# First-phase modulation in bursts of four tiles and raw transposes of x in a Hymba-style decoder block

## The chip, the cores and the metric

One core of a Trainium2 chip. The metric is the device time of one execution in microseconds, of the only core. All data is float32.

## The reference

One decoder layer on 256 tokens of width 2048. What matters here is its opening:

```python
mod = silu(c) @ W_ada + b_ada        # 6 x 2048: shift1, scale1, gate1, shift2, scale2, gate2
h   = RMSNorm(x, w1) * (1 + scale1) + shift1
u, q, k, v = split(h @ W_in)         # 1024 columns each
y_ssm = S5 diagonal SSM (64 groups of 16 channels, 64 states), GELU, GLU
y_att = QK-norm, dilated sliding-window attention with ALiBi (8 heads of 128)
x = x + gate1 * (concat(y_ssm, y_att) @ W_out)
x = x + gate2 * SwiGLU(RMSNorm(x, w2) * (1 + scale2) + shift2)
```

RMSNorm divides each token by the root of its mean square: one factor per row of x, which commutes with a transpose if it is then applied along the other axis.

## The kernel before

Every weight is read once, in tiles of 128 partitions x 1024 values (524,288 bytes), through one ring of six buffers (`raw`, line 105; `RAW = 6`). `load` (lines 104 to 107) takes the next ring buffer and issues the transfer on SyncE. SyncE's queue keeps the order in which the program issues; the other engines' orders are made ahead of the run by a scheduler that goes by program order and priorities (`tc.high_priority` moves a block forward). Once made, an engine's order is fixed.

A matmul weight is split into two parts, `whi` (ScalarE, line 131) and `wlo` (VectorE, line 133), and multiplied in three passes.

The opening, from the start to about 182 us, interleaves four things:

- The modulation of the first norm. `ada_stream` (lines 210 to 275) goes through sets p = 0 to 7; a set gives shift1 and scale1 for 256 channels and reads eight tiles, four of each kind. The tile is the moving operand and a four-column slice of silu(c) (`c7`) the weights (line 231). Tiles come in steps of two: load two, multiply both, yield. After the last step the sums go to SBUF (line 243), and after the first step of the next set `ada_finish` (lines 194 to 208) turns them into columns with four small matmuls (`adac`, line 199), adds bias and norm weight into `gcol` (lines 203 to 206) and calls `make_h(p)`. Sets of 512 columns, kinds 3 and 4 of the second norm, follow in the same stream.
- x. `x_norm` (lines 312 to 335): x lies in two tiles of the pool tag "x" (two buffers); sums of squares on ScalarE, 1/rms by a Newton iteration on VectorE (`rsqrt`, lines 89 to 100), both tiles scaled, then 32 transposes into PSUM (line 331) and eight copies of 128 x 512 into `xnT`.
- The projection. `make_h_(p)` (lines 588 to 596) makes 256 channels of h, transposed and in two parts, in a quarter of the pool tag "act" (four buffers, two p's each); `u_units` (lines 600 to 618) multiplies them with three tiles of W_in: two for u (line 608, into the PSUM tiles `uacc`) and one for the first half of q (line 150, `q0`).
- Constants and tables of the SSM on VectorE and ScalarE: `s5_consts` (line 354), `ssm_rot` (475) and `ssm_tables` (502), which need the transfer `bct <- bc` (line 668).

The main loop (lines 665 to 679) calls `ada` once in each turn n, steps the tables by a budget of 1.2 us, and from turn 9 on runs 1.45 units of the projection. A set takes eight turns, a p ten units. At turn 8 it fetches three tiles of W_in ahead, at turn 10 it issues bc:

```python
    for n in range(66):
        next(ada)
        if n == NBC:
            SP.dma_start(bct.rearrange("p a b c -> p (a b c)"), bc)
```

`U` takes one of x's two buffers (line 647) and is filled from `uacc` after p = 7 (`u_copy`, lines 649 to 654); `te` of `ssm_rot(2)` takes the other. Behind the opening come the rest of the in-projection with SSM and attention in between (to about 386 us), W_out, and the feed-forward part from about 523 us.

The second norm (lines 1026 to 1036) already uses the form of the change: `f = (x1T * g2) * rsw` with 1/rms as a row `rsw`, then Identity with a bias for the high part and one VectorE operation for the low part.

Of the kernel before, what the change touches and what calls it, by code (L numbers as in the profile page):

```python
# [7 lines left out]
F32 = mybir.dt.float32  # L8
F32R = mybir.dt.float32r
I32 = mybir.dt.int32  # L10
AF = mybir.ActivationFunctionType
ALU = mybir.AluOpType
# [3 lines left out]
D = 2048  # L16
# [45 lines left out]
def body(tc, sm, tabs, bc, brow, x, wada, wg2, win, wglu, wout, wgate, wup, wdown, out):  # L62
# [20 lines left out]
    A.dma_start(smt, sm)  # L83
    col = lambda n: smt[:, COLS[n][0]:COLS[n][1]]
# [89 lines left out]
    A.activation(cs, col("c"), AF.Tanh, scale=0.5)  # L174
    V.tensor_scalar(out=cs, in0=cs, scalar1=0.5, scalar2=0.5, op0=ALU.mult, op1=ALU.add)
    V.tensor_tensor(out=cs, in0=cs, in1=col("c"), op=ALU.mult)
    c7 = p1.tile([128, 16, 7], F32, name="c7")
    V.memset(c7, 0.0)
    V.tensor_copy(c7[:, :, 3], cs)  # L179
# [12 lines left out]
    h_hook = []  # L192

# [16 lines left out]
    def ada_stream(sets):  # L210

        pend = None
        for parts in sets:
            ps = ada_ps
            last = len(parts) - 1
            steps = []
            for i, (kind, g0, ng) in enumerate(parts):
                steps += [(i, h) for h in range(0, 2 * ng, 2)]
            w = parts[0][2] * 128
            nk = 1024 // w  # L220
            nt = 16 // nk
            seen = set()
            for n, (i, h) in enumerate(steps):
                kind, g0, ng = parts[i]
                base = kind * 4 + g0 // 4, (g0 % 4) // ng * nt + h
                wts = [load(wada[base[0], base[1] + t]).rearrange("p k n -> p (k n)") for t in range(2)]
                for t in (1, 0):
# [11 lines left out]
                if n < len(steps) - 1:  # L239
                    yield  # L240
# [66 lines left out]
    xt = [xp.tile([128, D], F32, name=f"x{t}", tag="x", bufs=2) for t in range(2)]  # L307
    for t in range(2):
        A.dma_start(xt[t], x[t])
    xnT = []  # L310

    def x_norm():
        ss1 = p1.tile([128, 2], F32, name="ss1")
        for t in range(2):
            junk = P8([128, D], "junk")
            A.activation(junk, xt[t], AF.Square, accum_out=ss1[:, t:t + 1])
            yield
        V.tensor_scalar(out=ss1, in0=ss1, scalar1=1.0 / D, scalar2=EPS, op0=ALU.mult, op1=ALU.add)
        rs1 = rsqrt(p1, ss1, 2, "a")
        yield  # L320
        V.tensor_scalar(out=xt[0], in0=xt[0], scalar1=rs1[:, 0:1], scalar2=None, op0=ALU.mult)
        A.mul(xt[1], xt[1], rs1[:, 1:2])
        yield
        for h in range(2):
            xn = P8([128, 8, 256], f"xnT{h}")
            for q in range(4):
                ps = ms([128, 2, 256], "tp")
                for k in range(2):
                    kc = h * 8 + q * 2 + k
# [3 lines left out]
                if q % 2:  # L333
                    yield
# [903 lines left out]
```

## Time and profile before

| what | us |
|---|---|
| median of 3 runs (lowest, highest) | 1264.25 (1263.53, 1267.47) |
| the profiled execution, its own time | 1264.14 |
| its span, first to last instruction | 1262.4 |
| TensorE busy in the span | 1216.4 |
| VectorE busy | 790.5 |
| ScalarE busy | 570.5 |
| mean granted TensorE clock | 0.996 |

The profile is one execution. The span is what the trace covers; the time of an execution has a little around it. Engines are PE (TensorE; PEld its weight loads), DVE (VectorE), ACT (ScalarE), POOL (GpSimd) and SP (SyncE, which issues transfers). A float32 matmul leaves two records. A line such as `L608 PE MATMUL uacc<-hT,whi` names the kernel's line, the engine, the operation, and its output and inputs. `[4.33 <-ACT hT L142]` says that the engine stood idle for 4.33 us before it and what ended the wait. Idle time of an engine that is not the bottleneck costs nothing.

### The profile page before, as it was taken

What the parts mean: (1) busy time and instruction counts of PE and PEld (TensorE: products, weight loads), DVE (VectorE), ACT (ScalarE), POOL (GpSimd) and SP (SyncE); (2) the same over time, 40 slices, a digit from 0 to 9 for tenths busy, and PEclk for the clock granted to TensorE, in tenths of its full rate; (3) what the DMA queues carried; (4) which work ended last, traced back from release to release, by engine and by line L of the source; (5) the groups of instructions that cost most, each with busy time, mean ns of one, the idle gap of its engine ahead of it and who ended that gap; (6) DMA issues with size and microseconds to landing.
All of it is one profiled execution on the core that took longest, in us unless ns stands there. A gap on an engine that the chain in (4) does not pass through costs nothing.

```text
span 1262.4 us, 18076 instructions
## 1 busy us (share of the span) xinstructions
PE 1216.4 (96%) x6884; PEld 965.2 (76%) x6884; DVE 790.5 (63%) x1389; ACT 570.5 (45%) x859; POOL 25.2 (2%) x50
## 2 busy tenths in 40 slices
PE   4888999999999999999999999999999999999998
PEld 2555667677789877688888888888888878888886
DVE  7894356667778989865655665665555444545443
ACT  3564373445455554554444444444434443333432
POOL 0210000000000000000000000000000000000000
PEclk9899999999999999999999999999999999999999
DMA  8788886777687799567777777777766556667662
GB/s 338 275 285 319 318 318 239 262 251 272 221 322 237 266 317 330 202 188 241 237 238 235 230 239 240 238 236 229 244 201 191 185 169 194 208 194 213 190 212 68
DMA packets 83032, 302.74 MB, mean 240 GB/s; under 512 B 9248, under 2 KB 9664, under 8 KB 82304
## 3 DMA queue, kind: packets, MB, share of 16 engines
q1 hardware_dynamic: 80784, 294.69, 70.4%
q10 hardware_dynamic: 1728, 4.38, 0.9%
q0 software_dynamic: 432, 2.51, 0.5%
q8 instruction: 54, 0.88, 0.3%
q14 instruction: 34, 0.28, 0.1%
HBM read 299.44 MB, written 2.10 MB: 239 GB/s over the span
## 4 chain that ended last, share of the span: by engine, by line
PE 80%; DVE 9%; DMA 6%; ACT 3%; issue 2%; SPq 0%; DVEq 0%; ACTq 0%
PE ff L150 38%; PE dn L150 14%; PE qkv L150 8%; PE dnl L150 5%; DMA raw<-wada 3%; PE ada L231 3%; PE uacc L608 3%; DVE wlo L133 2%; PE y L732 2%; DMA raw<-win 1%; DVE gate L268 1%; PE q L150 1%; PE y L728 1%; PE z L919 1%; PE S L698 1%
## 5 line engine op out<-in xcount | busy, mean ns | idle before, releaser
L133 DVE TENSOR_TENSOR wlo<-raw,whi 128x1024 fp32r<-128x1024 f32 x365 | 445.7, 1223 | 325.8 <-ACT whi L131 325.0
L131 ACT CAST whi<-raw 128x1024 fp32r<-128x1024 f32 x365 | 384.4, 1053 | 511.1 <-PE ff L150 268.6
L150 PE MATMUL ff<-whi,h2T 128*128 128x512 f32 x1408 | 437.2, 390 | 0.7 <-DVE h2T L1034 0.5
L150 PEld LDWEIGHTS ff<-whi,h2T 128*128 128x128 f32 x1408 | 264.0, 188 | 56.8 <-DVE h2T L1034 0.9
L150 PE MATMUL ff<-wlo,h2T 128*128 128x512 f32 x704 | 274.1, 389 | 0.0
L150 PE MATMUL dn<-whi,aT 128*128 128x512 f32 x528 | 163.4, 390 | 0.0
L150 PEld LDWEIGHTS ff<-wlo,h2T 128*128 128x128 f32 x704 | 132.2, 188 | 27.1
L150 PEld LDWEIGHTS dn<-whi,aT 128*128 128x128 f32 x528 | 99.1, 188 | 21.1 <-ACT whi L131 0.2
L150 PE MATMUL qkv<-whi,hT 128*128 128x512 f32 x320 | 107.4, 402 | 0.1
L150 PE MATMUL dn<-wlo,aT 128*128 128x512 f32 x264 | 103.1, 391 | 0.0
L231 PE MATMUL ada<-raw,c 128*4 128x256 f32 (+1 forms) x736 | 68.9, 470 | 16.1 <-DVE c L179 9.5
L150 PEld LDWEIGHTS qkv<-whi,hT 128*128 128x128 f32 x320 | 59.8, 188 | 25.1 <-issue 9.0
L1092 DVE SCALAR_TENSOR_TENSOR gate<-raw,cs,gate 128x1024 f32<-128x1024 f32 x32 | 41.1, 1285 | 56.5 <-DMA raw<-wg 56.5
L608 PE MATMUL uacc<-hT,whi 128*128 128x256 f32 x256 | 55.0, 308 | 9.4 <-ACT whi L131 4.9
L150 PE MATMUL qkv<-wlo,hT 128*128 128x512 f32 x160 | 63.6, 397 | 0.4 <-DVE wlo L133 0.4
L608 PEld LDWEIGHTS uacc<-hT,whi 128*128 128x128 f32 x256 | 42.5, 202 | 21.2 <-issue 9.5
L150 PEld LDWEIGHTS dn<-wlo,aT 128*128 128x128 f32 x264 | 49.6, 188 | 10.6 <-issue 0.5
L150 PE MATMUL dnl<-whi,aT 128*128 128x512 f32 x176 | 54.4, 389 | 0.0
L268 DVE SCALAR_TENSOR_TENSOR gate<-raw,cs,gate 128x512 f32<-128x512 f32 x64 | 47.8, 749 | 6.7 <-DMA raw<-wada 5.8
L231 PEld LDWEIGHTS ada<-raw,c 128*4 128x4 f32 x736 | 13.9, 87 | 42.5 <-issue 14.7
L608 PE MATMUL uacc<-hT,wlo 128*128 128x256 f32 x128 | 38.3, 300 | 1.1 <-DVE wlo L133 0.8
L150 PEld LDWEIGHTS dnl<-whi,aT 128*128 128x128 f32 x176 | 33.0, 188 | 7.0 <-DVE o L341 0.2
(312 smaller groups left out, 1262.1 us busy)
## 6 DMA issues: line engine op xcount, KB each, us to landing
raw<-wada SPq DMA_DIRECT2D x160, 512.0 KB, 5.3
raw<-wgate SPq DMA_DIRECT2D x88, 512.0 KB, 4.5
raw<-wup SPq DMA_DIRECT2D x88, 512.0 KB, 4.3
raw<-wdown SPq DMA_DIRECT2D x88, 512.0 KB, 4.3
raw<-win SPq DMA_DIRECT2D x64, 512.0 KB, 5.4
raw<-wout SPq DMA_DIRECT2D x32, 512.0 KB, 4.8
raw<-wg SPq DMA_DIRECT2D x32, 512.0 KB, 4.3
raw<-wglu SPq DMA_DIRECT2D x8, 512.0 KB, 4.8
```

Source lines behind the costliest of these rows:

```text
L131: A.copy(hi, raw)
L133: V.tensor_tensor(out=lo, in0=raw, in1=hi.bitcast(F32), op=ALU.subtract)
L150: PE.matmul(ps[t] if type(ps) is list else ps[:, t], lhsT=lhs(a, t), rhs=w[:, j], start=first and n == 0, stop=last and n == 2)
L231: PE.matmul(ps[32 * q:32 * q + 4, 0:w], lhsT=c7[:, kc, 3 - i:7 - i], rhs=wts[t][:, j * w:(j + 1) * w], start=q not in seen, stop=n == len( ...
L268: V.scalar_tensor_tensor(out=gb, in0=wt[:, j], scalar=cs[:, 2 * h + j:2 * h + j + 1], in1=gb, op0=ALU.mult, op1=ALU.add)
L608: PE.matmul(uacc[b][:, c], lhsT=wt[:, j, w], rhs=h[:, j, a], start=(kc == 0 and n == 0 and c % 2 == 0), stop=(kc == 15 and n == 2), skip_g ...
L698: PE.matmul(S[:, e, Q], lhsT=wv[:, 0, Q, e].rearrange("p i c -> p (i c)"), rhs=U[:, m, Q], start=True, stop=True)
L728: PE.matmul(yq[:, r], lhsT=T[:, Q, r], rhs=U[:, m, Q], start=r == 0, stop=False, skip_group_check=True, tile_position=(0, 32 * Q))
L732: PE.matmul(yq[:, r], lhsT=Vt[:, Q, e, r], rhs=hp[:, e, Q], start=False, stop=e == 1, skip_group_check=True, tile_position=(0, 32 * Q))
L919: PE.matmul(z[:, c], lhsT=wt[:, j, w], rhs=yT[kc // 4][:, kc % 4, a], start=(kc == 0 and n == 0 and c % 2 == 0), stop=(kc == 7 and n == 2) ...
L1092: V.scalar_tensor_tensor(out=g, in0=wt, scalar=cs[:, k:k + 1], in1=g, op0=ALU.mult, op1=ALU.add)
```

## The change

- The loads of x are issued right behind `smt`, ahead of the tanh on ScalarE's queue; silu(c) is made with high priority.
- A first-phase set takes its eight tiles in two steps of four instead of four steps of two, with the same eight turns. Of each four, two go through the ring, and the other two into one buffer of the tags "act" or "x" (`EXTRA`): "act" for the first step of sets 0 to 6 and the second step of sets 0 to 2, "x" for the second step of sets 3 to 7. The first step of set 7 takes four ring buffers. The matmuls of a step go from the last tile to the first.
- x is transposed as it came, through `uacc`, sixteen transposes at a time with four copies of 128 x 1024 in all; 1/rms becomes a row in all partitions (`rsx`) by two diagonal matrices, two matmuls with ones and a copy. `make_h_` applies it: two operations for the high part and one for the low part, for each of the two blocks of 128 channels.
- `U` is taken when `u_copy` first runs.

```diff
--- before.py
+++ after.py
@@ -81,6 +81,9 @@
 
     smt = const.tile([128, NSM], F32, name="smt")
     A.dma_start(smt, sm)
+    xt = [xp.tile([128, D], F32, name=f"x{t}", tag="x", bufs=2) for t in range(2)]
+    for t in range(2):
+        A.dma_start(xt[t], x[t])
     col = lambda n: smt[:, COLS[n][0]:COLS[n][1]]
     ident = col("id")
     ones = const.tile([128, 128], F32, name="ones")
@@ -171,12 +174,13 @@
 
 
     cs = const.tile([128, 16], F32, name="cs")
-    A.activation(cs, col("c"), AF.Tanh, scale=0.5)
-    V.tensor_scalar(out=cs, in0=cs, scalar1=0.5, scalar2=0.5, op0=ALU.mult, op1=ALU.add)
-    V.tensor_tensor(out=cs, in0=cs, in1=col("c"), op=ALU.mult)
     c7 = p1.tile([128, 16, 7], F32, name="c7")
     V.memset(c7, 0.0)
-    V.tensor_copy(c7[:, :, 3], cs)
+    with tc.high_priority(offset=HH):
+        A.activation(cs, col("c"), AF.Tanh, scale=0.5)
+        V.tensor_scalar(out=cs, in0=cs, scalar1=0.5, scalar2=0.5, op0=ALU.mult, op1=ALU.add)
+        V.tensor_tensor(out=cs, in0=cs, in1=col("c"), op=ALU.mult)
+        V.tensor_copy(c7[:, :, 3], cs)
     ada_ps = ms_p.tile([128, 512], F32, name="ada", bufs=1)
     V.memset(ada_ps, 0.0)
     sel = p1.tile([128, 4], F32, name="sel")
@@ -190,6 +194,13 @@
 
     MOD = {0: ("sh1", "bsh1", None), 1: ("g1", "bsc1", "w1"), 3: ("sh2", "bsh2", None), 4: ("g2", "bsc2", "w2")}
     h_hook = []
+
+    def EXTRA(si, n):
+
+        if n == 0 and si < 7:
+            return act, "act", 4
+        if n == 1:
+            return (act, "act", 4) if si < 3 else (xp, "x", 2)
 
     def ada_finish(parts, ev, whole=False):
         kind, g0, ng = parts[0]
@@ -210,21 +221,32 @@
     def ada_stream(sets):
 
         pend = None
-        for parts in sets:
+        for si, parts in enumerate(sets):
             ps = ada_ps
             last = len(parts) - 1
-            steps = []
-            for i, (kind, g0, ng) in enumerate(parts):
-                steps += [(i, h) for h in range(0, 2 * ng, 2)]
             w = parts[0][2] * 128
             nk = 1024 // w
             nt = 16 // nk
+            nb = 4 if nk == 4 else 2
+            steps = []
+            for i, (kind, g0, ng) in enumerate(parts):
+                steps += [(i, h) for h in range(0, nt, nb)]
             seen = set()
             for n, (i, h) in enumerate(steps):
                 kind, g0, ng = parts[i]
                 base = kind * 4 + g0 // 4, (g0 % 4) // ng * nt + h
-                wts = [load(wada[base[0], base[1] + t]).rearrange("p k n -> p (k n)") for t in range(2)]
-                for t in (1, 0):
+                wts = []
+                for t in range(nb):
+                    src = wada[base[0], base[1] + t]
+                    home = EXTRA(si, n) if nk == 4 and t >= 2 else None
+                    if not home:
+                        wts.append(load(src).rearrange("p k n -> p (k n)"))
+                        continue
+                    if t == 2:
+                        pr_ = home[0].tile([128, 2, 1024], F32, name="rawp", tag=home[1], bufs=home[2])
+                    SP.dma_start(pr_[:, t - 2], src)
+                    wts.append(pr_[:, t - 2])
+                for t in reversed(range(nb)):
                     for j in range(nk):
                         kc = (h + t) * nk + j
                         q = kc % 4
@@ -236,7 +258,7 @@
                     with tc.high_priority(offset=HH):
                         ada_finish(*pend)
                     pend = None
-                if n < len(steps) - 1:
+                for _ in range(nb - 1 if n < len(steps) - 1 else nb - 2):
                     yield
             ev = T2([128, 512], "adaev")
             with tc.high_priority(offset=HH):
@@ -304,35 +326,38 @@
         return next(ada, None) or 0.0
 
 
-    xt = [xp.tile([128, D], F32, name=f"x{t}", tag="x", bufs=2) for t in range(2)]
-    for t in range(2):
-        A.dma_start(xt[t], x[t])
     xnT = []
+    rsx = p2.tile([128, 256], F32, name="rsx", tag="hd", bufs=1)
 
     def x_norm():
+
         ss1 = p1.tile([128, 2], F32, name="ss1")
-        for t in range(2):
-            junk = P8([128, D], "junk")
-            A.activation(junk, xt[t], AF.Square, accum_out=ss1[:, t:t + 1])
+        for h in range(2):
+            xn = P8([128, 8, 256], f"xT{h}")
+            for t in range(2):
+                for i in range(2):
+                    for k in range(4):
+                        kc = h * 8 + i * 4 + k
+                        PE.transpose(uacc[i][:, k, t * 128:(t + 1) * 128], xt[t][:, kc * 128:(kc + 1) * 128], ident)
+                if h == 0:
+                    junk = P8([128, D], "junk")
+                    A.activation(junk, xt[t], AF.Square, accum_out=ss1[:, t:t + 1])
+                    yield
+            for i in range(2):
+                (V.tensor_copy if i else A.copy)(xn[:, 4 * i:4 * i + 4], uacc[i])
+            xnT.append(xn)
             yield
-        V.tensor_scalar(out=ss1, in0=ss1, scalar1=1.0 / D, scalar2=EPS, op0=ALU.mult, op1=ALU.add)
-        rs1 = rsqrt(p1, ss1, 2, "a")
-        yield
-        V.tensor_scalar(out=xt[0], in0=xt[0], scalar1=rs1[:, 0:1], scalar2=None, op0=ALU.mult)
-        A.mul(xt[1], xt[1], rs1[:, 1:2])
-        yield
-        for h in range(2):
-            xn = P8([128, 8, 256], f"xnT{h}")
-            for q in range(4):
-                ps = ms([128, 2, 256], "tp")
-                for k in range(2):
-                    kc = h * 8 + q * 2 + k
+            if h == 0:
+                with tc.high_priority(offset=HH):
+                    V.tensor_scalar(out=ss1, in0=ss1, scalar1=1.0 / D, scalar2=EPS, op0=ALU.mult, op1=ALU.add)
+                    rs1 = rsqrt(p1, ss1, 2, "a")
+                    rb = ms([128, 256], "rb")
                     for t in range(2):
-                        PE.transpose(ps[:, k, t * 128:(t + 1) * 128], xt[t][:, kc * 128:(kc + 1) * 128], ident)
-                (A.copy if TPC[q % 2] else V.tensor_copy)(xn[:, 2 * q:2 * q + 2], ps)
-                if q % 2:
-                    yield
-            xnT.append(xn)
+                        dg = T2([128, 128], "dgx")
+                        V.tensor_scalar(out=dg, in0=ident, scalar1=rs1[:, t:t + 1], scalar2=None, op0=ALU.mult)
+                        PE.matmul(rb[:, t * 128:t * 128 + 128], lhsT=ones, rhs=dg, start=True, stop=True)
+                    A.copy(rsx, rb)
+                yield
 
 
     def SC(n, w=32):
@@ -591,8 +616,12 @@
         tmp = T2([128, 2, 256], "htmp")
         for k in range(2):
             kc = p * 2 + k
-            ts(tmp[:, k], xnT[kc // 8][:, kc % 8], gcol["g1"][:, kc:kc + 1], gcol["sh1"][:, kc:kc + 1], ALU.mult, ALU.add)
-        split(hT[-1][:, p % 2 * 2:p % 2 * 2 + 2], tmp)
+            h = hT[-1][:, p % 2 * 2 + k]
+            sh = gcol["sh1"][:, kc:kc + 1]
+            V.scalar_tensor_tensor(out=tmp[:, k], in0=xnT[kc // 8][:, kc % 8], scalar=gcol["g1"][:, kc:kc + 1], in1=rsx,
+                                   op0=ALU.mult, op1=ALU.mult)
+            A.activation(h[:, 0], tmp[:, k], AF.Identity, bias=sh)
+            V.scalar_tensor_tensor(out=h[:, 1], in0=tmp[:, k], scalar=sh, in1=h[:, 0].bitcast(F32), op0=ALU.add, op1=ALU.subtract)
         units.append(u_units(p, hT[-1][:, p % 2 * 2:p % 2 * 2 + 2]))
 
     h_hook.append(make_h)
@@ -644,10 +673,13 @@
 
     st_ = start()
     tab_gen = tabs_early()
-    U = xp.tile([128, 8, 4, 64], F32, name="U", tag="x", bufs=2)
+    U_ = []
 
     def u_copy(b):
 
+        if not U_:
+            U_.append(xp.tile([128, 8, 4, 64], F32, name="U", tag="x", bufs=2))
+        U = U_[0]
         for Q in range(4):
             for i in range(4):
                 src = uacc[b][32 * Q:32 * Q + 32].rearrange("p m (j i) -> p m i j", i=4)[:, :, i]
@@ -684,6 +716,7 @@
         unit()
 
     yT = [P8([128, 4, 2, 256], f"yT{i}", F32R) for i in range(2)]
+    U = U_[0]
 
 
     def ssm_batch(m):
```

## Rows read from the trace of the kernel before

**Rows 1.** TensorE's busy tenths in the span's 40 slices, from the page.

```profile
PE   4888999999999999999999999999999999999998
```

**Rows 2.** Stages: length; PE, PEld, DVE, ACT, POOL busy (instructions); clock, DMA share, GB/s.

```profile
0.00:38.00 38.00, 17.89 (x132) 8.10 (x132) 28.62 (x175) 13.46 (x17) 6.20 (x21) 0.99 0.89 338
38.00:51.00 13.00, 12.94 (x90) 10.63 (x90) 10.52 (x35) 5.64 (x28) 1.85 (x2) 0.77 0.60 231
51.00:101.00 50.00, 42.52 (x400) 28.69 (x399) 46.70 (x151) 34.44 (x72) 4.95 (x7) 1.00 0.82 285
101.00:182.00 81.00, 73.57 (x633) 51.08 (x632) 30.08 (x61) 35.10 (x68) 3.10 (x5) 0.98 0.91 328
182.00:500.00 318.00, 314.24 (x2269) 244.86 (x2269) 246.59 (x546) 161.35 (x336) 8.61 (x14) 1.00 0.77 272
```

**Rows 3.** Timeline of TensorE: start, us, line, operation [idle before it <- releaser].

```profile
14.89 1.89 PE L231 MATMUL ada<-raw,c 128*4 128x256 f32 x16 [3.46 <-DMA raw<-wada]
...
38.06 0.80 PE L608 MATMUL uacc<-hT,whi 128*128 128x256 f32 x2 [4.33 <-ACT hT L142]
...
160.48 0.54 PE L199 MATMUL adac<-sel,adaev 128*128 128x2 f32 x4
```

**Rows 4.** Chain of waits up to 200 us: start, us, what.

```profile
0.74 4.49 DMA smt<-sm
...
131.82 6.41 DMA raw<-wada
...
156.47 7.74 DMA raw<-win
```

**Rows 5.** SyncE's waits up to 182 us: total us, times, longest.

```profile
SPq L106 <- PE ada L231: 80.4, 40, 6.7
```

**Rows 6.** Short stretches, columns as in rows 2.

```profile
20.00:25.00 5.00, 3.88 (x25) 1.00 (x21) 3.58 (x26) 2.16 (x2) 0.00 (x0) 1.00 1.03 410
40.00:45.00 5.00, 5.00 (x29) 5.00 (x28) 5.00 (x14) 4.48 (x23) 0.79 (x1) 0.60 0.55 224
120.00:125.00 5.00, 3.48 (x17) 3.27 (x18) 1.50 (x2) 1.75 (x2) 0.00 (x0) 0.75 1.02 401
```

**Rows 7.** Timeline of SyncE and VectorE.

```profile
28.74 0.96 SPq L668 DMA_DIRECT2D bct<-bc  x1
...
39.92 0.42 DVE L344 TENSOR_SCALAR bct<-bct 128x512 f32<-128x512 f32 x1
...
51.73 0.16 DVE L203 TENSOR_TENSOR sh<-adac,smt 128x2 f32<-128x2 f32 x1 [3.14 <-PE adac L199]
```

**Rows 8.** Groups by line and form: count | busy us, mean ns | idle before.

```profile
L143 DVE TENSOR_TENSOR hT<-htmp,hT 128x512 fp32r<-128x512 f32 x8 | 5.5, 688 | 1.4 <-ACT hT L142 1.4
L1033 ACT ACTIVATE h2T<-h2f,sh 128x256 fp32r<-128x256 f32 x12 | 5.4, 500 | 0.7 <-DVE h2f L1030 0.7
...
L1030 DVE SCALAR_TENSOR_TENSOR h2f<-x1T,g,rsw 128x256 f32<-128x256 f32 x12 | 5.2, 479 | 0.0
...
L142 ACT CAST hT<-htmp 128x512 fp32r<-128x512 f32 x8 | 5.0, 620 | 10.8 <-DVE htmp L346 10.8
...
L332 DVE COPY xnT<-tp 128x512 f32<-128x512 f32 x4 | 2.8, 692 | 3.9 <-PE tp L331 3.9
```

**Rows 9.** Instructions of line 346: ns minimum/median/maximum, first and last start.

```profile
L346 DVE TENSOR_SCALAR htmp<-xnT,g,sh x16: 395/411/2057, 35.0 to 162.0; 128x256 f32<-128x256 f32 x16
```

**Rows 10.** Timeline of TensorE around one burst.

```profile
45.68 0.28 PE L608 MATMUL uacc<-hT,wlo 128*128 128x256 f32 x1
45.89 1.05 PE L231 MATMUL ada<-raw,c 128*4 128x256 f32 x16
...
47.20 0.28 PE L608 MATMUL uacc<-hT,wlo 128*128 128x256 f32 x1
```

**Rows 11.** Timeline of TensorE at 120 and 138 us.

```profile
120.76 0.51 PE L608 MATMUL uacc<-hT,whi 128*128 128x256 f32 x2 [1.01 <-ACT whi L131]
...
138.28 1.05 PE L231 MATMUL ada<-raw,c 128*4 128x256 f32 x16 [0.75 <-DMA raw<-wada]
```

## The prediction

> **What bounds the kernel now.** I read the slices of the page first: TensorE is at nine tenths or more almost everywhere, less only in the first slices [rows 1]. So a change confined to the opening is worth what it takes out of the opening's gaps. The busy time by stage gives their size [rows 2]: TensorE is busy 17.89 of the first 38 us, 12.94 of the next 13, 42.52 of 50 (51 to 101) and 73.57 of 81 (101 to 182); in the 318 us behind, 314.24. Nothing after 182 us is edited, so I carry what 0 to 182 gives through to the end; its cover is the engine that is full there.
>
> The parts of the opening have different limits. From 0 to 38 us the first projection matmul waits for the modulation of set 0, for x and for its weights: it starts at 38.06 after 4.33 us of empty TensorE [rows 3]. From 51 to 101 VectorE is the wall, 46.70 of 50 us busy, by the tables of the SSM [rows 2]. From 101 to 182 VectorE has 30.08 of 81, DMA's share is 0.91, and the chain of waits holds transfers of 6.41 and 7.74 us [rows 2, 4]: TensorE frees a ring buffer, SyncE issues, and TensorE is back before the tile has landed. SyncE waits 80.4 us of the opening for the modulation matmuls [rows 5].
>
> **Part 1: the start.** The sixteen DMA engines are full in the four slices from 5 to 25 us, at 410 GB/s in the one shown [rows 6]; a 524,288-byte tile then takes 1.28 us. The second burst of before waited until 14.89 for tiles 2 and 3 [rows 3]; by then four tiles and most of x had come. The change asks for the same bytes by its first burst of four, so I put it at 14.6; that cs is ready sooner, and that x's second half leaves ahead of the tanh, gives nothing, since these bytes decide. Tiles 4 to 7 land by 14.6 + 4 x 1.28 = 19.7, 8 to 11 by 24.8. SyncE runs ahead, because second pairs take no ring buffers: its first W_in issue needs only the buffer of tile 0 (free at about 16.6), so the three W_in tiles land at 26.1, 27.4 and 28.7, and bc (1 MB, two tiles) at 31.2. Before, bc was issued at 28.74 [rows 7].
>
> The x side no longer stands in front: gone are two scalings of x, eight copies (VectorE's four of 0.692) and the wait for 1/rms ahead of 32 transposes; four copies of twice the width come in, two on VectorE. No row shows one: below, 0.69 (as if width were free), above, 2 x 0.69 = 1.38; I take 1.2, nearer the top, since each moves what two did [rows 8]. The sums of squares and the chain of small operations for 1/rms, both as before, follow x's landing by some 6 us, so they are done near 20, before the modulation of set 0 is (second burst 19.7 to 21.7). So the first projection matmul waits for the first W_in tile and its cast, about 1 us: 27.1, 10.9 us earlier, with the same twelve modulation tiles done. The half-clock stretch goes too: after the 4.33 us gap the slice from 40 to 45 was granted 0.60, that is 1.2 GHz for most of it [rows 6], and VectorE got set 1's result at 51.73 [rows 7]. Now the last four tiles of set 1 land at 31.2 + 4 x 1.28 = 36.3; burst and reduction close it at 39.9: 11.8 us earlier for TensorE.
>
> VectorE, the wall that follows, moves less. It was busy 28.62 of the first 38 us [rows 2] and came to bc at 39.92 [rows 7]. Two copies of 1.2 for four of 0.692 and the lost scaling (four times a copy's width of work, about 1.3) leave 27.0; its constants begin when smt lands, 5.23 [rows 4], so without idle time it is at the tables at 32.2, with 1 us idle at 33: 6.9 us earlier. TensorE's 11.8 is the upper bound. Before, it also stood still 3.14 us for the adac of set 1 [rows 7], which now comes 11.8 us sooner. I take 8.5, towards the 6.9, because VectorE is the later of the two. Below, if its fixed order keeps its idle time, it could be 2.
>
> **Part 2: the new make_h** costs VectorE four operations of 0.479 (the second normalisation's rows of this shape and formula) for two of 0.411 (the median) and one of 0.688: 1.92 - 1.51 = 0.41 us for each p; ScalarE 2 x 0.50 - 0.62 = 0.38 [rows 8, 9]. Four p's fall before 101 us, where VectorE is the path: 4 x 0.41 = 1.6 us lost. The other four are covered by VectorE's free 51 us of 81, ScalarE's by its free 46 of 81 [rows 2]; without these covers 1.6 more. The first matmul of a p needs 0.48 + 0.50 instead of 0.82 + 0.62, so 0.46 less; I count nothing, since units of the p before fill that wait.
>
> **Part 3: bursts of four.** The matmuls stay; a change-over goes. The last projection record ahead of a burst starts at 45.68 (spacing 0.12), the burst at 45.89, and the third projection record behind it at 47.20, so a burst of 16 takes 47.20 - 0.24 - 45.80 = 1.16 us out of the stream, 0.09 of it the gap in front [rows 10]. No row shows a burst of 32. At worst a merger saves nothing; if the gap behind and the filling of the array are shared too, perhaps 0.3. I take 0.22, since the gap in front has an equal behind. Sixteen mergers, but it counts only where TensorE sets the pace: six or seven (sets 5 to 7 and the edge of set 4), 1.5 us; bounds 0 and 16 x 0.3 = 4.8.
>
> **Part 4: the deeper queue.** Of a set's eight wada and three W_in tiles seven pass through the six ring buffers now, not eleven; the others use hT's and x's empty places. So SyncE can be 6/7 of a set ahead instead of 6/11. Every issue is still there, 64 + 24 on SyncE's queue. A second pair waits for its home, and what is behind it on that queue (the next W_in) waits too; but the home's last reader is a burst two or three earlier, in sets 5 and 6 one whole set, so I cost that at nothing; without that cover, a landing of 6.41 [rows 4] in a set. What can be won from 101 to 182 are the transfers that TensorE felt: 1.01 and 0.75 us empty at 120 and 138 [rows 11], the slow stretch behind the first (0.75 of the clock from 120 to 125, 1.3 us [rows 6]), and part of the waits for casts; some 5. TensorE idles 81 - 73.57 = 7.4 there, so at most 7.4 + 1.3 = 8.7. I take 3, because a burst needs its third and fourth tile two turns sooner, which eats part of the depth; below 0, or a loss (third rival).
>
> U takes its place in x's buffers only at the first u_copy, after the last burst there, so it waits for nothing new.
>
> **The sum.** 8.5 - 1.6 + 1.5 + 3 = 11.4 us. Against the profiled execution (1264.14 us, span 1262.4 and 1.7 around it; the median of three runs, 1264.25, is 0.1 away): 1252.7, say 1253. A difference under 0.3%, 3.8 us, is taken as no change.
>
> **A rule against it.** The trace: the granted clock fell to 1.2 GHz after 4.33 us without a matmul, and again around 120, where a wait of 1.01 stands among others; it stayed at 2.4 through the many short waits from 51 to 101 [rows 2, 3, 6, 11]. The Trainium skill, "TensorE: Matmul & The Clock Gate", section "HAM oscillation — how this bites in real kernels", says that short bursts separated by long waits for DMA make each burst start cold. By that rule the change, which gathers two short waits into a long one, would end as the third rival; the rows agree for the longest gap only, as projection units lie between bursts.
>
> The Trainium skill, "DMA: Bandwidth & Descriptors", section "Where 436 GB/s comes from", puts the HBM limit of one core near 358 GB/s; 410 in [rows 6] disagrees, and the measurement decides. By the page a tile takes 1.46 us, an estimate, bc lands 2 us later, and the sum would be up to 2 us less.
>
> **The rivals.**
> *All waits go.* If VectorE is no wall (its order merely follows TensorE's), the whole 11.8 stays, with mergers at 3.5 and 6 of the 8.7: 21.3 us, 1243. For: TensorE idles 7.5 us from 51 to 101; against: VectorE's 46.70 of 50. Chance 0.22.
> *VectorE swallows the start.* The tables end at 101 as they did: -1.6 + 1.5 + 3 = 2.9, 1261, no change. For: 93% busy; against: its work itself can begin 7 us earlier. Chance 0.12.
> *The bursts of four wait, and run cold.* Slower. Place: the fourteen bursts of sets 1 to 7. A burst that catches up with its transfers waits for two tiles more, 2 x 1.28 = 2.6 us, and the clock falls as at 120, 1.3 more: 3.9 each. It decides from four bursts on (15.6 against 11.4); at seven of fourteen, 27.3 - 11.4 = 16 us slower, 1280. For: DMA's share 0.91 and the 4.33 us case; against: the deeper queue, and ten units of each p between. Chance 0.07.
> *The second pair finds no place earlier*, so the queue is as short as before: the 3 is gone, and what is behind it waits for one landing, 6.4: 1262. Chance 0.04.
> The forecast itself has 0.55: 1253, between 1248 and 1259.
>
> **How the numbers follow.** Faster by over 0.3% (under 1260.3): 0.55 + 0.22 and a third of the second and fourth rival, 0.82. No change: the rest of these two, 0.11. Slower: 0.07. The range holds the forecast, half of the first rival (from 1244) and the two near no change (to 1262).
>
> **What would show it.** Right: first burst near 14.6, first projection matmul near 27, no half-clock stretch around 40, bc landed by 32, the tables done near 93, adac of set 7 (160.48 before [rows 3]) at 147 to 151, the stages after 182 as long as before. Wrong: the tables still ending at about 101 (second rival), adac of set 7 before 141 (first), bursts that wait for wada with 1.2 GHz behind them (third), SyncE waiting for readers of hT or x (fourth), or a shift gained early and given back after 182.

## The result and the profile after

The changed kernel takes 1253.89 us (median of 4 runs, 1251.80 to 1254.58) against 1264.42 for the kernel before in the same measurement; the ratio is 0.9912, with a 95% interval of 0.9888 to 0.9935. The profiled execution of after took 1254.49 us, its span 1252.7. The forecast was 1253.0. The total came out as predicted; most of what stood behind it did not.

First the slices of the page of after, TensorE's busy tenths, as in [rows 1]:

```profile
PE   4789899999999999999999999999999999999998
```

Then the stage windows, columns as in [rows 2]:

```profile
0.00:38.00 38.00, 18.59 (x155) 12.30 (x156) 29.05 (x187) 12.79 (x19) 5.78 (x17) 0.96 0.97 379
38.00:51.00 13.00, 9.86 (x86) 7.64 (x85) 12.58 (x38) 5.91 (x21) 1.84 (x2) 1.00 0.79 298
51.00:101.00 50.00, 43.76 (x426) 33.13 (x425) 33.33 (x99) 31.40 (x70) 6.33 (x9) 0.93 0.83 287
101.00:182.00 81.00, 74.69 (x646) 53.92 (x645) 48.78 (x125) 47.18 (x107) 2.44 (x7) 1.00 0.86 320
182.00:500.00 318.00, 314.89 (x2260) 246.18 (x2260) 247.59 (x538) 158.67 (x315) 8.63 (x14) 1.00 0.78 274
```

VectorE's load from 51 to 101 us fell from 46.70 to 33.33 and rose from 30.08 to 48.78 behind it. No step of the prediction had that. The column of the clock shows 1.00 also where no clock was recorded, as at the start of a trace (see "Half clock" below). TensorE's timeline of after (start, us, line, operation, idle before):

```profile
15.20 1.89 PE L253 MATMUL ada<-rawp,c 128*4 128x256 f32 x16 [2.78 <-DVE ss_tb L369]
16.86 1.94 PE L253 MATMUL ada<-raw,c 128*4 128x256 f32 x16
...
22.01 1.75 PE L341 MATMUL uacc<-smt,x 128*128 128x128 f32 x14 [1.32 <-DVE xT L347]
23.70 1.05 PE L253 MATMUL ada<-rawp,c 128*4 128x256 f32 x16
...
31.10 0.50 PE L637 MATMUL uacc<-hT,whi 128*128 128x256 f32 x2 [1.62 <-ACT whi L134]
34.47 0.58 PE L637 MATMUL uacc<-hT,wlo 128*128 128x256 f32 x1 [2.87 <-DVE wlo L136]
...
48.30 0.61 PE L210 MATMUL adac<-sel,adaev 128*128 128x2 f32 x4 [2.06 <-ACT adaev L265]
...
100.95 0.40 PE L637 MATMUL uacc<-hT,whi 128*128 128x256 f32 x2
101.28 1.05 PE L253 MATMUL ada<-rawp,c 128*4 128x256 f32 x16
102.14 1.05 PE L253 MATMUL ada<-raw,c 128*4 128x256 f32 x16
103.12 0.39 PE L637 MATMUL uacc<-hT,wlo 128*128 128x256 f32 x1
103.34 0.40 PE L637 MATMUL uacc<-hT,whi 128*128 128x256 f32 x2
...
148.22 0.54 PE L210 MATMUL adac<-sel,adaev 128*128 128x2 f32 x4
```

The first projection matmul, at 38.06 before, comes at 31.10. But the matmuls behind it waited 2.87 us for a cast of VectorE and 2.06 for a copy of ScalarE, and the second group of projections (p = 1) starts at 55.83, where it was 55.63, with two more modulation tiles done ahead of it. The seven us were gone. By the first projection matmul of p = 3 (93.89; before 95.70) the lead is 1.8, by p = 5 (122.71; 131.69) it is 9.0, and it stays: the remaining in-projection begins at 171.38 instead of 181.79, and from there to the end of the span it is 1081.3 us, before 1080.6. So the whole gain seems to lie between 94 and 140 us, nowhere near the place that the largest term named.

### The profile page after: what moved, and what is told of

Read it like the earlier page. It is cut to its first block, busy times and chain, and to the rows that moved or that the text cites. A ratio compares the mean times of both kernels' runs of the same rounds, so it can differ in the third digit from the quotient of the medians.

```text
span 1252.7 us, 18073 instructions
## 1 busy us (share of the span) xinstructions
PE 1207.4 (96%) x6888; PEld 967.0 (77%) x6888; DVE 790.9 (63%) x1396; ACT 570.7 (46%) x865; POOL 25.5 (2%) x50
## 4 chain that ended last, share of the span: by engine, by line
PE 79%; DVE 10%; DMA 6%; ACT 3%; issue 2%; SPq 0%; POOL 0%; DVEq 0%; ACTq 0%; POOLq 0%
PE ff L153 38%; PE dn L153 14%; PE qkv L153 8%; PE dnl L153 5%; DMA raw<-wada 3%; PE ada L253 3%; PE uacc L637 2%; DVE wlo L136 2%; PE y L765 2%; DMA raw<-win 2%; DVE gate L290 1%; PE S L731 1%; PE y L761 1%; PE q L153 1%; PE atp L1147 1%
## 5 line engine op out<-in xcount | busy, mean ns | idle before, releaser
L637 PE MATMUL uacc<-hT,whi 128*128 128x256 f32 x256 | 51.6, 300 | 6.9 <-ACT whi L134 6.9
L253 PE MATMUL ada<-raw,c 128*4 128x256 f32 (+1 forms) x496 | 50.6, 492 | 0.1
L153 PEld LDWEIGHTS qkv<-wlo,hT 128*128 128x128 f32 x160 | 30.1, 188 | 6.4 <-DVE rsyq L102 0.9
```

The source lines that it names most:

```text
L153: PE.matmul(ps[t] if type(ps) is list else ps[:, t], lhsT=lhs(a, t), rhs=w[:, j], start=first and n == 0, stop=last and n == 2)
L253: PE.matmul(ps[32 * q:32 * q + 4, 0:w], lhsT=c7[:, kc, 3 - i:7 - i], rhs=wts[t][:, j * w:(j + 1) * w], start=q not in seen, stop=n == len( ...
L637: PE.matmul(uacc[b][:, c], lhsT=wt[:, j, w], rhs=h[:, j, a], start=(kc == 0 and n == 0 and c % 2 == 0), stop=(kc == 15 and n == 2), skip_g ...
```

## The experiments

Twelve kernels were run. Two words are used below: a *home* is a buffer of the tags "act" or "x" that takes a second pair (`EXTRA`), and a *merger* makes one burst of two. One table first; in it "clock" is the mean granted TensorE clock of a kernel's runs, "lost" is (1 - clock) x span, and the last column is the mean time without the lost part. It is an account, not a measurement; how far it holds is tested below.

| kernel | ratio to before, 95% | median us | clock | lost us | mean less lost |
|---|---|---|---|---|---|
| before (78 runs) | 1 | 1263.7 to 1266.1 | 0.9946 | 6.8 | 1258.2 |
| after | 0.9912, 0.9888 to 0.9935 | 1253.89 | 0.9942 | 7.2 | 1246.3 |
| x_only | 1.0008, 0.9989 to 1.0026 | 1265.88 | 0.9892 | 13.7 | 1252.3 |
| hold_te | 1.0012, 0.9995 to 1.0030 | 1267.17 | 0.9937 | 8.0 | 1258.8 |
| no_x_homes | 0.9976, 0.9957 to 0.9994 | 1261.03 | 0.9918 | 10.3 | 1251.3 |
| bursts_only | 0.9928, 0.9906 to 0.9950 | 1255.29 | 0.9942 | 7.2 | 1248.1 |
| no_x_hold | 0.9978, 0.9960 to 0.9996 | 1262.24 | 0.9917 | 10.5 | 1251.4 |
| pairs_with_homes | 1.0009, 0.9992 to 1.0026 | 1266.31 | 0.9877 | 15.6 | 1250.5 |
| ring4 | 1.0013, 0.9995 to 1.0031 | 1266.70 | 0.9907 | 11.8 | 1254.5 |
| wide4 | 0.9903, 0.9884 to 0.9923 | 1253.19 | 0.9924 | 9.5 | 1244.9 |
| x_only_warm | 0.9970, 0.9951 to 0.9989 | 1262.21 | 0.9958 | 5.4 | 1256.8 |
| after_warm | 0.9928, 0.9906 to 0.9950 | 1257.00 | 0.9930 | 8.8 | 1248.8 |
| tb08 | 1.0106, 1.0082 to 1.0129 | 1277.00 | 0.9878 | 15.5 | 1261.8 |
| wide4_tb08 | 1.0060, 1.0040 to 1.0081 | 1271.92 | 0.9875 | 15.9 | 1255.7 |

**The first four: which part, and is VectorE the wall?** Reading the two traces had given a rival. Of x's two buffers, which `te` of the third rotation took early before, the second steps' tiles now take turns in both; GpSimd's first write to `te` moved from 32.71 to 113.05 us, and some 14 us of VectorE's work with it. The row, from GpSimd's timeline of after:

```profile
113.05 0.11 POOL L510 MEMSET te<- 128x8 f32 x1 [13.64 <-PE ada L253]
```

*x_only*, after without bursts of four and homes:

```diff
-            nb = 4 if nk == 4 else 2
+            nb = 2
...
-                    home = EXTRA(si, n) if nk == 4 and t >= 2 else None
+                    home = None
```

> The changed kernel with bursts of two and no second pairs in hT's and x's places: only the x part, the earlier silu(c) and the new make_h are left. The prediction's account (start +8.5, make_h -1.6): 6.9 us under before, about 1257.5, first projection matmul near 31 and the gain still there at 94 us. The rival account (VectorE is full from 25 to 75 us, so an earlier start is given back behind it; the gain came later, because te of the third rotation got its x buffer only at 113 us and its tables left the full stretch): te is early again here, so 1263 to 1266, the lead at the first matmul of p = 0 some 7 us and by p = 3 under 2.

*hold_te*, before with the third rotation made dependent on set 6:

```diff
-        G.memset(E[:, 0, :, 0:1], 1.0)
+        if mp == 2:
+            V.tensor_scalar(out=E[:, 0, :, 0:1], in0=gcol["g1"][:, 6:14].unsqueeze(2), scalar1=0.0, scalar2=1.0, op0=ALU.mult, op1=ALU.add)
+        else:
+            G.memset(E[:, 0, :, 0:1], 1.0)
```

> The kernel before, with one edit: the third rotation's first instruction reads set 6's g1, so its VectorE work can't start before about 130 us. The prediction's account knows no such term: 1264, within 2 us. The rival account: 14 to 18 us of VectorE work leave the stretch from 51 to 101 us (46.70 busy there, about 32 to be seen) and go behind it, where there is room; TensorE's 7.5 us of idle time there shrink: 1258 to 1261. If the tables become late for the SSM behind 182 us, slower than before.

*no_x_homes*, after:

```diff
-            return (act, "act", 4) if si < 3 else (xp, "x", 2)
+            return (act, "act", 4) if si < 3 else None
```

> The changed kernel, but the second steps of sets 3 to 7 take ring buffers, not x's. So te of the third rotation gets x's buffer early again, and nine tiles of a late set pass through the ring instead of seven. The prediction's account: half of the 3 us for depth goes, 1255 to 1256, te without influence. The rival account: the third rotation is back in VectorE's full stretch (51 to 101 us near 45 busy), so 3 to 6 us are lost beside the depth: 1257 to 1261, and set 7's adac at 152 to 157.

*bursts_only*: the kernel before with after's `EXTRA`, `ada_stream` and late `U`, and nothing else of the diff.

> The kernel before with the bursts of four and their second pairs in hT's and x's places, U taken late, but x scaled, transposed and used by make_h as before. The prediction's account: mergers 1.5 and depth 3, so 4.5 us under before, 1260 (the homes in x's place come only from set 3 on). The rival account: late te, mergers of 0.29 and depth without the start, which it holds to be worth nothing: 1253 to 1257, no slower than the changed kernel by more than 2 us.

The stage from 51 to 101 us of hold_te, same columns:

```profile
51.00:101.00 50.00, 42.46 (x407) 29.30 (x404) 34.89 (x100) 31.38 (x64) 5.75 (x8) 1.00 0.82 287
```

VectorE lost 11.8 us of work there (46.70 to 34.89), and TensorE did 42.46 us, 42.52 before [rows 2]; the time did not fall (1.0012). From the first projection matmul to that of p = 3 it takes 57.60 us, and before 57.64 (38.06 [rows 3] to 95.70):

```profile
36.10 0.58 PE L611 MATMUL uacc<-hT,whi 128*128 128x256 f32 x1 [3.76 <-ACT hT L142]
...
93.70 0.39 PE L611 MATMUL uacc<-hT,whi 128*128 128x256 f32 x1 [0.80 <-ACT whi L131]
```

VectorE was no wall, so neither the prediction's reading of this stage nor the rival's holds. The 36.10 says one thing more: hold_te opens as before does, so some 2 us of the start differ from one execution to another. x_only is no faster than before either, with its first projection matmul at 33.94; pairs_with_homes, below, has it at 30.04, the earliest of all, and is no faster either. So the start alone is worth nothing. bursts_only gives nearly all (0.9928; the intervals can't tell it from 0.9912), with its first projection matmul at 31.43: the early start, too, came with the bursts, without the new x part. And no_x_homes, with the same edits but for x's places, keeps only 3 us of the 11.

**The next four: depth, mergers, te.** *no_x_hold* is no_x_homes with the edit of hold_te. *ring4* is after with `home = None` (as in x_only, bursts of four kept). *pairs_with_homes* is after with every second pair at home (the indices of the pair's buffer follow):

```diff
-            nb = 4 if nk == 4 else 2
+            nb = 2
...
-                    home = EXTRA(si, n) if nk == 4 and t >= 2 else None
+                    home = EXTRA(si, n // 2) if nk == 4 and n % 2 else None
...
```

*wide4* is after with the second norm's sets in fours, through the ring:

```diff
-            nb = 4 if nk == 4 else 2
+            nb = 4
...
-                                  start=q not in seen, stop=n == len(steps) - 1 and (nk == 2 or t == 0))
+                                  start=q not in seen, stop=n == len(steps) - 1 and t * nk < 4)
```

> The kernel no_x_homes (the second steps of sets 3 to 7 through the ring) with the late start of the third rotation from hold_te. If x's places pay because they keep te and its tables out of VectorE's full stretch (the rival account): as fast as the changed kernel, ratio to before 0.990 to 0.993. If they pay because the queue is deeper (the prediction's part 4): no better than no_x_homes, ratio 0.996 to 0.999, and the stage from the projection of p = 3 to the end of p = 7 stays near 82 us (77.5 in the changed kernel, 86.1 before).

> The changed kernel in bursts of two again, with every second pair still in hT's or x's place: the same depth, the same late te, no merger. The prediction's account: mergers 1.5, so 1255 to 1256. The rival account, in which mergers save 0.29 each and all sixteen count: 1258 to 1259. If depth is nearly all of it: within 1 us of the changed kernel, ratio to before near 0.992.

> The changed kernel with bursts of four, all from the six ring buffers: mergers without depth, te early. The prediction's account: 3 us less than the changed kernel gains, so 1256 to 1257. If depth is most of it: 1262 to 1266, since with four of six buffers in one burst SyncE can be only a step ahead; the waits of SyncE for modulation matmuls above 80 us, and TensorE waiting for wada tiles. If mergers are most of it: 1258 to 1260.

> The changed kernel, and the sets of the second norm too in bursts of four tiles, through the ring: sixteen more mergers behind 182 us, where TensorE is busy 314.9 of 318 us. If a merger saves 0.22 to 0.29 wherever TensorE sets the pace: 3.5 to 4.6 us under the changed kernel, 1249 to 1251. If four of six buffers in one burst leave the queue too short there: slower than the changed kernel, TensorE waiting for wada or W tiles behind 182 us.

no_x_hold equals no_x_homes (0.9978, 0.9976), so the move of `te` is worth nothing and x's places pay by depth: from p = 3 to the end of p = 7 it takes 83.1 us (no_x_homes 83.0, after 77.5). But depth without mergers (pairs_with_homes, 1.0009) gives nothing, and mergers without depth (ring4, 1.0013) nothing. ring4's reason is in TensorE's waits from 101 to 182 us:

```profile
PE ada L253 <- DMA raw<-wada: 7.4, 4, 3.5
```

After has 1.1 there. With four of six buffers in one burst the transfers come late. But before has no more than after, so the depth took no wait for tiles away; it keeps the bursts of four from waiting. The lines of before and of after:

```profile
PE ada L231 <- DMA raw<-wada: 0.8, 1, 0.8
...
PE ada L253 <- DMA rawp<-wada: 1.1, 1, 1.1
```

For pairs_with_homes, whose queue is as deep as after's, there is no such line. Its stage windows show another thing, in the column of the granted clock:

```profile
0.00:38.00 38.00, 23.02 (x169) 14.79 (x170) 29.17 (x189) 13.13 (x20) 5.78 (x17) 0.87 0.97 384
38.00:51.00 13.00, 9.52 (x88) 6.40 (x88) 12.47 (x35) 6.98 (x22) 1.84 (x2) 1.00 0.91 311
51.00:101.00 50.00, 41.54 (x360) 29.09 (x361) 32.96 (x95) 27.99 (x59) 5.02 (x7) 0.90 0.73 265
101.00:182.00 81.00, 73.95 (x621) 52.78 (x621) 40.33 (x106) 37.63 (x81) 3.74 (x9) 0.92 0.80 294
```

**Half clock.** x_only has the same. Short windows over its slow stretches:

```profile
25.00:40.00 15.00, 9.96 (x52) 7.87 (x53) 13.62 (x75) 5.70 (x12) 0.86 (x1) 0.54 0.62 235
52.00:60.00 8.00, 6.50 (x44) 4.84 (x48) 7.89 (x23) 6.33 (x12) 0.95 (x1) 0.57 0.88 338
66.00:70.00 4.00, 3.88 (x20) 3.65 (x19) 4.00 (x12) 1.61 (x3) 0.00 (x0) 0.57 0.74 257
124.00:132.00 8.00, 7.02 (x40) 5.16 (x41) 2.45 (x2) 1.62 (x3) 0.00 (x0) 0.57 0.66 238
145.00:149.00 4.00, 4.00 (x34) 3.26 (x30) 0.00 (x0) 0.00 (x0) 0.00 (x0) 0.57 0.97 362
```

A clock of 0.57 over 8 us is 2 x 0.43 x 8 = 6.9 us at 1.2 GHz, the rest at 2.4. The five lines add up to 34 us. In front of four of them stand waits of TensorE (timeline of x_only):

```profile
28.60 1.22 PE L358 MATMUL rb<-dgx,ones 128*128 128x128 f32 x4 [5.42 <-DVE dgx L357]
...
65.36 0.50 PE L637 MATMUL uacc<-hT,whi 128*128 128x256 f32 x2 [1.34 <-ACT whi L134]
...
124.25 0.54 PE L637 MATMUL uacc<-hT,whi 128*128 128x256 f32 x2 [2.91 <-ACT whi L134]
...
143.99 1.05 PE L253 MATMUL ada<-raw,c 128*4 128x256 f32 x16 [1.82 <-DMA raw<-wada]
```

The kernel before has 10 us of it up to 182, at 36 to 45 and 122 to 126; after has 10 too, at 33 to 38, 51 to 55 and 85 to 90; pairs_with_homes, by the windows above, 33. TensorE's waits of 1 us and more from 25 to 182 us are 5 in before, 6 in after, 8 in pairs_with_homes, 9 in x_only; but no_x_homes has 6 too, at a lower clock (0.9918). The kept traces overstate the contrast: those of x_only and pairs_with_homes are the slowest of their ten executions (0.986), those of before and after have a clock of 0.996. By the mean clocks of all executions (twice the lost column) it is 14 us in before and after, 27 in x_only, 31 in pairs_with_homes. And it is not one execution: x_only's ten runs have clocks of 0.986 to 0.992, those of before 0.991 to 0.997. Within x_only the time follows the clock, from 1261.82 us at 0.991 to 1270.94 at 0.986; over the seven kernels with ten or more runs in the first two series (before among them), a fitted line gives 0.66 to 1.06 us of time for each us lost by the clock, each slope uncertain by 0.1 to 0.4. So the last column of the table, which counts 1 us for each, is a rough account, and by it the start is there after all: x_only is 5.9 us better than before (1258.2 - 1252.3; with a slope of 0.66 it would be 3.6) and loses 6.9 more at half clock (13.7 - 6.8).

The account has a hole at the start. Ahead of a trace's first clock record the windows show 1.00, but there a burst of sixteen takes 1.89 us, as one does at 30.80 in x_only, within the first stretch above, and 1.05 later. In before the change lies between these two lines, in after between 16.86 and 23.70 (shown above):

```profile
20.89 1.89 PE L231 MATMUL ada<-raw,c 128*4 128x256 f32 x16 [0.68 <-DMA raw<-wada]
...
32.68 1.05 PE L231 MATMUL ada<-raw,c 128*4 128x256 f32 x16
```

TensorE's busy time ahead of the first record is 14.5 us in before (to 30.36), 7.4 in after (to 20.66), 7.6 in x_only (to 18.77) and 9.0 in hold_te, which opens as before does (to 24.49). So up to 3.5 us of x_only's 5.9 may be a shorter beginning at half speed, and part of that only the difference of two executions; no run separates them.

That was argued from traces. *x_only_warm* tests it: x_only with matmuls that nobody reads, in the waits of TensorE. *after_warm* does the same to after.

```diff
+                for f in range(WARM.get((si, n), 0) if nk == 4 else 0):
+                    PE.matmul(ps[32 * (f % 4):32 * (f % 4) + 4, 256:512], lhsT=c7[:, f % 16, 3:7], rhs=wts[0][:, 0:256],
+                              start=True, stop=True, skip_group_check=True)
                 yield
...
                     rb = ms([128, 256], "rb")
+                    for _ in range(9):
+                        PE.matmul(rb, lhsT=ones, rhs=xn[:, 7], start=True, stop=True)
```

`WARM` is {(1,0): 6, (1,3): 14} in x_only_warm and {(1,0): 20, (1,1): 14}, without the nine, in after_warm. In both, the added matmuls write with start flags beside the running sums of set 1, and set 1's modulation is then no longer whole, as far as can be told; the rest of the work is that of the kernels they start from.

> The kernel x_only with matmuls that nobody reads put where TensorE stood idle in it: nine of 128x256 ahead of the two for the row of 1/rms (5.42 us idle before it), six behind set 1's first burst and fourteen behind its last (1.88 and 1.01 us idle). The clock account (x_only's earlier start is worth about 6 us, and is given back because TensorE spends 34 us at 1.2 GHz in its profiled run where the kernel before has 10): the mean clock rises from 0.989 to 0.992 to 0.995 and the time falls by 3 to 6 us, to 1259 to 1262, ratio to before about 0.996. The rival (half clock is only how waiting looks; the waits themselves cost the time): the clock may rise, the time stays at 1264 to 1267, or is longer by the added matmuls.

> The changed kernel with matmuls that nobody reads where TensorE waits in its first 52 us: twenty behind set 1's first burst (1.62 us idle, then 2.87) and fourteen behind its second (2.06, 0.41, 0.68). The clock account: the half-clock stretches at 34 to 38 and 51 to 55 us go or become shorter, 1.7 us each, so up to 3.4 us under the changed kernel, 1250 to 1253. The rival (the stage is paced by VectorE, full from 25 to 75 us): the stretches go, the time stays within 1 us of the changed kernel, 1253 to 1255.

x_only_warm's clock rose from 0.9892 to 0.9958, and its time fell from 1.0008 to 0.9970 of before, 4.8 us of 1265 (uncertain by 3.3), as the clock account expected; the lost part fell by 8.3 us. Where the difference went was not separated. Its first window, for comparison with x_only's 0.54:

```profile
25.00:40.00 15.00, 12.46 (x127) 9.40 (x126) 14.50 (x52) 8.23 (x22) 4.19 (x8) 1.00 0.80 316
```

The test is not pure: the scheduler also moved the row of 1/rms ahead of x's second half in it. The row's matmuls start at 23.65, without the 5.42 us of wait at 28.60 in x_only, and TensorE's idle time up to the remaining in-projection is 29.2 us instead of 38.4. So the gain fits the clock account, but it can as well come from the waits that went; that half clock costs the time is argued, not shown. In after_warm the stretch at 34 us went, another one grew behind (48 to 55), the mean clock did not rise (0.9930, after 0.9942), and the time did not fall (0.9928). The expectation missed at its first step, so the run says nothing on what a higher clock would give.

**Two tries to beat both.** *tb08* is after with `TB = 0.8` instead of 1.2, *wide4_tb08* is wide4 with the same.

> The changed kernel with the tables of the SSM stepped by a budget of 0.8 us a turn instead of 1.2, so that less of VectorE's and ScalarE's work stands ahead of the casts, the modulation's columns and make_h from 25 to 100 us, and more behind 101 us, where VectorE is busy 48.8 of 81. If VectorE's queue sets the waits of 2.87 (low part of the first W_in tile) and 2.06 (copy of set 1's sums) and the half clock behind them: these waits shrink, clock up, 2 to 5 us under the changed kernel, 1249 to 1252. If TensorE's own work and DMA set the pace from 51 us on, as the held third rotation suggested: within 1 us of the changed kernel. Slower, if the tables come late for the SSM behind 171 us.

> The same with the second norm's sets in bursts of four too (wide4). If the sixteen mergers behind 182 us are worth their 0.29 each on top: 3 to 4.6 us under tb08. If, as wide4 itself leaves open (0.9903 against 0.9912), they are eaten by waits for tiles: equal to tb08 within 1.5 us.

Both are slower than before. The first casts were no earlier (the waits of 2.87 stayed), the first projection matmul of p = 1 waits 4.83 us for a cast (0.59 in after), the remaining in-projection of tb08 begins at 175.82, 4.4 us later than in after, and from there to the end it is 1100.3 us instead of 1081.3. The largest wait of TensorE there, from 300 to 500 us, has no counterpart in after; that the late tables cause it was not tested:

```profile
PE qtp L817 <- ACT qn L805: 6.9, 1, 6.9
```

wide4_tb08 is 5.1 us better than tb08 at the same clock (0.9875, 0.9878). The wait above is 5.6 us in it, 1.3 less; the other 3.8 would be sixteen mergers at 0.24. wide4 itself, with the same mergers, can't be told from after (0.9903 to 0.9912): its clock was lower (0.9924), and in its profile, which is the slowest of its five executions, TensorE waits 3.1 us for tiles of wada behind 182 us, where after does not. No version was found that is measurably better than the changed kernel.

## Why the prediction was right, and where it was not

**What bounds the kernel.** "VectorE is the wall" from 51 to 101 us is the step that failed first. 46.70 of 50 busy was read as a limit; hold_te took 11.8 us away and TensorE did not notice. What paces the stage instead is TensorE's own work with its short waits, as far as these runs show.

**Part 1, 8.5 us: failed as a term.** The start moved by 7.0 us, not 10.9, and had gone again at p = 1. Set 1's `adac`, which was to end at 39.9, starts at 48.30 (before 51.19): its second burst of four comes at 44.34 without a wait in front, because TensorE's order has projection matmuls there. Of its details the first burst held (15.20 for 14.6); the second came at 23.70 instead of 19.7, since it stood behind transposes that waited for a copy; VectorE reached bc at 39.00, where 33 was forecast and 39.92 had been. "The half-clock stretch goes too" was wrong: the half clock moved, and stayed at 10 us. Alone (x_only) the part is worth nothing; by the account it buys as much half clock as it saves otherwise, and without the lost clock it is worth 5.9 us, near the 8.5 - 1.6 of the sum, with the hole named above. Beside the bursts it adds at most a little (bursts_only 0.9928, after 0.9912).

**Part 2, -1.6: the durations held, the place not.** The operations, by group and form in after (count | busy us, mean ns | idle):

```profile
L623 ACT ACTIVATE hT<-htmp,sh 128x256 fp32r<-128x256 f32 x16 | 7.3, 502 | 12.5 <-DVE htmp L621 12.5
L624 DVE SCALAR_TENSOR_TENSOR hT<-htmp,sh,hT 128x256 fp32r<-128x256 f32 x16 | 7.1, 482 | 0.9 <-ACT hT L623 0.7
L621 DVE SCALAR_TENSOR_TENSOR htmp<-xT,g,rsx 128x256 f32<-128x256 f32 x16 | 7.0, 479 | 0.1
...
L347 DVE COPY xT<-uacc 128x1024 f32<-128x1024 f32 x2 | 2.4, 1224 | 3.6 <-PE uacc L341 3.6
```

482, 502 and 479 ns answer to the 479 and 500 of [rows 8]; the copy of twice the width took 1.22 for an estimate of 1.2. Since VectorE was not on the path, the 1.6 was charged to an engine that had room.

**Part 3, 1.5: too small.** By the method of [rows 10], the last projection record ahead of the burst at 101 us starts at 101.07, so the next was due at 101.19; the third behind it starts at 103.46, so the first was due at 103.22. A burst of 32 takes 2.03 us out of the stream, two of 16 took 2.32. A merger saves 0.29, predicted 0.22, bound 0.3. The larger miss is the count: pairs_with_homes against after, clock left out, is 4.2 us (16 x 0.26), so all sixteen seem to count and not six or seven; with no wall of VectorE nothing hides them. The other sixteen, behind 182 us, fit 3.8 of the 5.1 that wide4_tb08 gained on tb08.

**Part 4, 3 us: wrong in what it would win, and mis-sized by its dependence on part 3.** "The transfers that TensorE felt" did not go (0.8 us of waits for tiles from 101 to 182 us, after 1.1). "A burst needs its third and fourth tile two turns sooner, which eats part of the depth" was the right worry. ring4 prices it: bursts of four without the homes lose 1.01% against after (1.0013 - 0.9912), 12.8 us, above the bound of 8.7; 4.6 of them are lost clock (11.8 - 7.2). Depth for bursts of two is worth 1.8 us without the lost clock (1252.3 - 1250.5), and nothing with it.

**The sum.** Without the lost clock the three come to 5.9 + 1.8 + 4.2 = 11.9 us, forecast 6.9 + 3 + 1.5 = 11.4. But they are steps of one chain (before, x_only, pairs_with_homes, after) and add up to the whole by construction; by another chain bursts_only is worth 10.1 and the x part 1.8 behind it. So the agreement of the total is in good part luck: the terms were mis-sized in both directions. Nor do the steps add as measured: x_only, pairs_with_homes and ring4 are worth nothing, and only bursts of four with homes end with the clock that the kernel had before. The time therefore hung on a condition which the prediction's sum took as given, that the half clock would not grow. Most single parts broke it.

**The rivals.** "All waits go" did not come: idle time of TensorE up to the remaining in-projection is 34.8 us, before 35.1. So the 10.4 us won up to there are not idle time at all: TensorE is busy 136.6 us instead of 146.7. Of these 10.1 an estimate puts 4.6 on the sixteen mergers (0.29 each), 3.6 on the shorter beginning at half speed (half of 14.5 - 7.4) and 1.0 on four matmuls of the SSM that come behind that point now; the last 0.9 is not accounted for. "VectorE swallows the start" is what the start looks like at p = 1, but its cause fell with hold_te. "Bursts of four wait and run cold" is what ring4 does, without the homes: 7.4 us of waits, clock 0.9907, no change instead of slower. The rule quoted from the Trainium skill, "TensorE: Matmul & The Clock Gate", section "HAM oscillation — how this bites in real kernels", did not speak against bursts of four as such: bursts of two lost more (0.9892 and 0.9877). The checkpoints for set 7's `adac` (147 to 151, measured 148.22) and for the stages behind held, and could not tell the right terms from wrong ones. "The tables done near 93" did not: the third rotation's work on `te` starts only at 113.05.

**Open.** Why waits of about the same length are followed by half clock in one place (1.34 us at 65 in x_only) and not in another (1.54 at 79.65), and so why the pairs lose more than the bursts, is not settled. Pairs with homes, and bursts of four without them, were not tried without the x part. What moves most of the gain to the stretch from p = 3 to p = 5 was not separated further.

## What to carry to other kernels

An engine that is 93% busy in a stage is a suspect, not the bound: take some of its work away before building a sum on it. A gain need not be idle time: here TensorE waited as long as before, and its busy time shrank. Before two versions of a kernel whose TensorE is 96% busy are compared, read their mean granted clock: a part that shortens one long wait but adds several short ones may lose by the clock what it wins. And test parts that share a queue together as well as alone; here three kernels with a part left out (x_only, pairs_with_homes, ring4) gained nothing, and the whole gained 0.9%.

## What was not expected of the hardware

The same program ran with a mean granted clock from 0.986 to 0.992 (x_only, ten runs, 1261.82 to 1270.94 us) and another from 0.991 to 0.997 (before). With twenty-nine added matmuls, each over 128x256 values in float32, and the order that the scheduler then chose, x_only became faster by 4.8 us. And an edit of the order alone, for the same bytes and homes, changes how long TensorE is granted 2.4 GHz: by the mean clocks 31 us at half clock with pairs at home, 14 with fours at home. A trace's granted clock says nothing ahead of its first record: there a burst took 1.89 us under a shown clock of 1.00, and 1.05 later.
